# FFN-down on one Trainium2 core: column sums formed by transfers into a ring, and 8, 8, 8, 5 seven-product blocks in place of 7, 7, 7, 4

## The chip, the cores and the metric

The kernel runs on one core of one Trainium2 chip. The metric is the device time of a run in microseconds (us), the median of several runs. Three runs of the kernel before gave 1180.41, 1181.60 and 1181.63 us. A separate execution was taken by the hardware profiler; every time of an instruction below is from that one.

## The reference

One layer of a decoder trunk on 256 tokens of width 2048, in float32. The change lies in the channel mixer, a squared-ReLU MLP with a hidden width of 8192:

```python
h2 = rms_norm(x, mlp_norm[i])
x = x + jnp.square(jax.nn.relu(h2 @ w_ffn_up[i])) @ w_ffn_down[i]
gate = jax.nn.sigmoid(rms_norm(x, ple_norm[i]) @ w_ple_gate[i])
x = x + gate * (p[i] @ w_ple_proj[i])
```

What is timed is the whole layer; what is changed is the product with `w_ffn_down`, (256 x 8192) by (8192 x 2048).

## The kernel before

**Precision.** TensorE multiplies in a reduced float32 format (fp32r). Each operand is therefore split into a high part, its rounding (ScalarE, ACT below), and a low part, the rest (VectorE, DVE below: operand minus high part). A product is three matmuls: high by high, high by low, low by high. `split_sb` (L172, L173) does this for 512 columns, `halves_of` (L1240, L1241) for a panel of 1024: two ACT instructions of 512 columns and one DVE instruction of 1024. Their results are called `wh_...` and `wl_...`, or `wad` for one tile that holds both parts.

**Tiling of FFN-down.** The hidden width is worked in two halves (`hf`), the output width in two halves of 1024 columns (`pair`), so there are four *sweeps*, called d00, d01, d10, d11 by `hf` and `pair`. d00 and d01 follow each other, then comes the up-product of the second half, then d10 and d11. A sweep makes 16 *visits* (`kp`), each to 256 hidden rows: two row tiles of 128, by two column blocks of 512. With the two token tiles of 128 a visit is a product of 2 x 2 blocks. The weight blocks are w11, w12 (first row tile, column blocks one and two), w21, w22 (second row tile). The activations are a11, a12, a21, a22.

- A *plain* visit makes the usual eight block products, 24 matmuls of 128 x 512 (`prod`, L1229 to L1231).
- A *square* makes seven products, 21 matmuls, by Winograd's form of Strassen's scheme. For it the DVE forms four sums of the weight blocks (L1269 to L1272: t1 = w12 - w11, t3 = w22 - w12, t2 = t3 + w11, t4 = w21 - t2, in a tile `td`), and sums of the activations (s1 to s4, in `S`, made once per half in `activation_sums`). Their split parts are the tiles `..b` (w21, w22), `..c` (t1, t3), `..d` (t2, t4) and `wad` (w11) of a visit, `11b` being tile b of visit 11.

Before, the squares are the visits 1, 3, 5, 7, 9, 11, 13 of three sweeps and 1, 3, 7, 11 of the last. The seven products are collected in eight PSUM banks, and at the last square some of them are added to the residual stream `xr` by the DVE (`add`, L1249); four more banks are added at the sweep's end.

**Buffers and queues.** A visit loads two panels of 512 KB (`load_raw`, L158, names `raw_d...`), issued on SyncE's queue (SP) in order. Six buffers hold panels: a load waits until the last reader of an earlier panel has ended. The split parts go to three buffers `wh` and `wl` (`..a`, `..b`, `..c`), two buffers for `..d`, and one for `wad`; they come free when TensorE (PE) has made the last matmul that reads them. The order of the instructions on each engine is written out by a scheduler at build time, with `tc.high_priority` around the splits; at run time each engine takes its list strictly in order.

Of the kernel before, what the change touches and what calls it, by code (L numbers as in the profile page):

```python
# [9 lines left out]
F32 = mybir.dt.float32  # L10
F32R = mybir.dt.float32r
# [29 lines left out]
def trunk(  # L41
# [1114 lines left out]
    def inv_ms():  # L1156
        ss2 = rms_stat(xr, "n2")
        nc.vector.tensor_scalar(s2, ss2, 1.0 / D, NORM_EPS, op0=ALU.mult, op1=ALU.add)
        nc.vector.reciprocal(s2, s2)

    h3_box = []

# [22 lines left out]

    SEVEN = (1, 3, 5, 7, 9, 11, 13)
    s_slots = (0, 2, 5)

    def activation_sums(box, kp, r):

        i = SEVEN.index(kp)
        if i % 2 == 0:
            st = a8(s_slots[i // 2], f"S{kp}", F32R) if i < 6 else fp.tile([128, 1024], F32R, tag="S", name=f"S{kp}")
            box[kp] = box[SEVEN[min(i + 1, len(SEVEN) - 1)]] = st
# [5 lines left out]
        nc.vector.tensor_tensor(s3, a11, a21, op=ALU.subtract)  # L1202
# [4 lines left out]
    def down_sweep(hf, pair, ys, sboxes, hooks=(), between=None, seven=SEVEN):  # L1207

        nm = f"d{hf}{pair}"
        hooks = dict(hooks)  # L1210
# [12 lines left out]
        left = dict(todo)  # L1223

        def prod(n, a_, w_):
            first, last = left[n] == todo[n], left[n] == 1
            left[n] -= 1
            (ah, al), (wh, wl) = a_, w_
            nc.tensor.matmul(banks[n], ah, wh, start=first, stop=False)  # L1229
            nc.tensor.matmul(banks[n], ah, wl, start=False, stop=False)  # L1230
            nc.tensor.matmul(banks[n], al, wh, start=False, stop=last)  # L1231

        def halves_of(src, name, own=False):

            pool, kw = (fp, dict(bufs=2)) if own else (wp, {})
            wh = pool.tile([128, 1024], F32R, tag="graw" if own else "wh", name=f"wh_{name}", **kw)
            wl = pool.tile([128, 1024], F32R, tag="graw" if own else "wl", name=f"wl_{name}", **kw)
            with tc.high_priority(20000):
                for c in range(2):
                    nc.scalar.activation(wh[:, c * 512 : c * 512 + 512], src[:, c * 512 : c * 512 + 512], AF.Copy)  # L1240
                nc.vector.tensor_tensor(wl, src, wh.bitcast(F32), op=ALU.subtract)  # L1241
# [6 lines left out]
        def add(tt, c, src):  # L1248
            nc.vector.scalar_tensor_tensor(xs(tt, c), src, s2[:, tt : tt + 1], xs(tt, c), op0=ALU.mult, op1=ALU.add)  # L1249

        for q, kp in enumerate(((0, 2, 1, 4, 3, *range(5, 16)) if hf else (0, 2, 1, 4, 3, 6, 5, 8, 7, 10, 9, 12, 11, 14, 13, 15)) if pair else range(16)):
            if q in hooks:
                hooks[q]()
            y, j = ys[kp // 2], kp % 2 * 512
            a11, a21, a12, a22 = ((y[:, j + i * 128 : j + i * 128 + 128], y[:, 1024 + j + i * 128 : 1152 + j + i * 128]) for i in range(4))
            rx, ry = (load_raw(w_down[pair, hf * 32 + 2 * kp + i], 1024, f"{nm}_{kp}_{i}") for i in range(2))
            if kp in seven:
                i = SEVEN.index(kp)
                st = sboxes[kp][:, i % 2 * 1024 : i % 2 * 1024 + 1024]
                s1, s2_, s3, s4 = ((st[:, c * 128 : c * 128 + 128], st[:, 512 + c * 128 : 640 + c * 128]) for c in range(4))  # L1260
                t_ = a8(1, f"t{nm}_{kp}")
                t1, t3, t2, t4 = (t_[:, c * 512 : c * 512 + 512] for c in range(4))
                wa = fp.tile([128, 1024], F32R, tag="wa", name=f"wa{nm}_{kp}")
                w11 = wa[:, 0:512], wa[:, 512:1024]
                with tc.high_priority(20000):
                    split_sb(*w11, rx[:, 0:512])
                w21, w22 = halves_of(ry, f"{nm}_{kp}b")
                with tc.high_priority(20000):
                    nc.vector.tensor_tensor(t1, rx[:, 512:1024], rx[:, 0:512], op=ALU.subtract)  # L1269
                    nc.vector.tensor_tensor(t3, ry[:, 512:1024], rx[:, 512:1024], op=ALU.subtract)  # L1270
                    nc.vector.tensor_tensor(t2, t3, rx[:, 0:512], op=ALU.add)
                    nc.vector.tensor_tensor(t4, ry[:, 0:512], t2, op=ALU.subtract)  # L1272
                w1, w3 = halves_of(t_[:, 0:1024], f"{nm}_{kp}c")
                w2, w4 = halves_of(t_[:, 1024:2048], f"{nm}_{kp}d", True)
                for n, a_, w_ in (("1", a11, w11), ("2", a12, w21), ("3", s4, w22), ("5", s1, w1), ("7", s3, w3), ("6", s2_, w2), ("4", a22, w4)):
                    prod(n, a_, w_)
            else:
                w11, w12 = halves_of(rx, f"{nm}_{kp}a")
                for n, a_, w_ in (("2", a11, w11), ("4", a21, w11), ("3", a11, w12), ("x", a21, w12)):
                    prod(n, a_, w_)  # L1280
                w21, w22 = halves_of(ry, f"{nm}_{kp}b")
                for n, a_, w_ in (("2", a12, w21), ("4", a22, w21), ("3", a12, w22), ("x", a22, w22)):
                    prod(n, a_, w_)
            if kp == seven[-1]:
                u = fp.tile([128, 512], F32, tag="r", bufs=2, name=f"u{nm}")
                with tc.high_priority(20000):
                    add(0, 0, b1)
                    nc.scalar.activation(u, b1, AF.Copy)
                    nc.vector.tensor_tensor(u, b6, u, op=ALU.add)
                    add(0, 1, b5)  # L1290
                    add(1, 1, b5)
                    add(0, 1, u)
                    nc.vector.tensor_tensor(u, b7, u, op=ALU.add)
                add(1, 0, u)
                add(1, 1, u)
                if between is not None:
                    between()
        for n, tt, c in (("2", 0, 0), ("4", 1, 0), ("3", 0, 1), ("x", 1, 1)):
            with tc.high_priority(30000):
                add(tt, c, banks[n])  # L1300

    def ffn_half(hf):
# [26 lines left out]
        if hf == 0:  # L1329
            down_sweep(hf, 1, ys, sboxes)  # L1330
        else:
            down_sweep(hf, 1, ys, sboxes, {5: keep, 8: keep, 11: keep, 14: keep}, lambda: [h3_part("ple_norm", n) for n in range(2)], (1, 3, 7, 11))
            for n in range(2, 4):
                h3_part("ple_norm", n)

    ffn_half(0)
    ffn_half(1)
    h3 = h3_box[0]


    praw = load_raw(pT.rearrange("p a t -> p (a t)"), 512, "pT")
    ph, pl = (fp.tile([128, 512], F32R, tag=nm, name=nm) for nm in ("ph", "pl"))
    split_sb(ph, pl, praw[:, 0:512])
    pp = [a8(1 + tt, f"pp{tt}") for tt in range(2)]
    for n in range(4):
# [74 lines left out]
def _layout(i):  # L1420
# [13 lines left out]
    def ktiles(w):  # L1434
# [30 lines left out]
        "w_ffn_down": a["w_ffn_down"][0].reshape(64, 128, 2, 1024).transpose(2, 0, 1, 3),  # L1465
# [24 lines left out]
```

## Time and profile before

| what | value |
|---|---|
| median of three runs | 1181.6 us |
| the profiled execution, its device time | 1180.25 us |
| span of the profile | 1178.2 us |
| PE busy | 1162.5 us, 99% |
| DVE busy | 873.3 us, 74% |
| ACT busy | 709.3 us, 60% |
| moved by DMA | 216.81 MB |

The profile lists, for each engine, when every instruction ran, how long, and what ended the idle time before it. "PEld" is the weight load of TensorE, which runs beside the matmuls. "x365" is a count of instructions. A matmul's row gives 0.39 us, but the next one starts before it ends, so its cost is read from one start to the next. The same is done for the DVE and ACT, whose rows overlap a little too.

### The profile page before, as it was taken

The page shows a single profiled execution, that of the slowest core. Times are in us where ns is not written, and L with a number is a line of the kernel's source. Part 1 is how long each engine was busy: PE and PEld are TensorE (multiplying, and loading weights), DVE is VectorE, ACT ScalarE, POOL GpSimd, SP SyncE. Part 2 cuts the span into 40 slices and gives each one's busy share as a digit, 9 for nine tenths or more (in the row PEclk, how much of TensorE's full clock was granted, in tenths as well). Part 3 has the DMA queues.
Part 4 walks back from the last instruction along what each step waited for, and adds up shares of the span by engine and source line. Part 5 has one row for each costly group of instructions (what it writes and reads, how often), then busy time and mean ns, then how long its engine had stood idle before and what let it go on. Part 6 is the DMA issues. An engine that isn't in the chain of part 4 may idle for free.

```text
span 1178.2 us, 17287 instructions
## 1 busy us (share of the span) xinstructions
PE 1162.5 (99%) x6419; PEld 973.4 (83%) x6419; DVE 873.3 (74%) x1188; ACT 709.3 (60%) x1309; POOL 13.7 (1%) x73
## 2 busy tenths in 40 slices
PE   8999999999999999999999999999999999999997
PEld 8787777788887888888888888888888888888886
DVE  7786996964656666767988987676668879788543
ACT  7776848676545565555665664555556655568543
POOL 2100000000000000000000000000000000000000
PEclk9999999999999999999999999999999999999999
DMA  7464343354465555555556556555555555767511
GB/s 290 154 202 146 135 140 119 119 179 157 160 203 178 177 182 196 184 192 200 187 204 212 198 202 209 186 191 191 185 195 190 202 205 195 290 233 249 197 56 72
DMA packets 60756, 216.81 MB, mean 184 GB/s; under 512 B 6784, under 2 KB 7552, under 8 KB 60288
## 3 DMA queue, kind: packets, MB, share of 16 engines
q1 hardware_dynamic: 60240, 214.99, 52.5%
q8 instruction: 50, 0.82, 0.3%
q10 hardware_dynamic: 432, 0.73, 0.2%
q14 instruction: 34, 0.28, 0.1%
HBM read 213.59 MB, written 2.10 MB: 183 GB/s over the span
## 4 chain that ended last, share of the span: by engine, by line
PE 96%; ACT 1%; DVE 1%; DMA 0%; issue 0%; SPq 0%; POOL 0%; DVEq 0%; POOLq 0%
PE u_w L1112 20%; PE u_w L1117 10%; PE d_b L1231 7%; PE d_b L1229 7%; PE d_b L1230 7%; PE d_w L1231 2%; PE d_w L1229 2%; PE d_w L1230 2%; PE gt_b L242 2%; PE gt_b L241 2%; PE gt_b L238 2%; PE zk_b L241 1%; PE zk_b L242 1%; PE o_b L241 1%; PE o_b L242 1%; PE zv_b L238 1%
## 5 line engine op out<-in xcount | busy, mean ns | idle before, releaser
L1112 PE MATMUL u_w<-h,wh_u 128*128 128x512 f32 x1024 | 321.9, 395 | 0.0
L167 ACT ACTIVATE wh_u<-raw_u 128x512 fp32r<-128x512 f32 x256 | 147.5, 623 | 160.9 <-issue 98.2
L168 DVE TENSOR_TENSOR wl_u<-raw_u,wh_u 128x1024 fp32r<-128x1024 f32 x128 | 156.6, 1224 | 105.2 <-ACT wh_u L167 103.5
L1117 PEld LDWEIGHTS u_w<-h,wl_u 128*128 128x128 f32 x1024 | 192.4, 188 | 45.4
L1117 PE MATMUL u_w<-h,wl_u 128*128 128x256 f32 x1024 | 201.4, 278 | 0.0
L1112 PEld LDWEIGHTS u_w<-h,wh_u 128*128 128x128 f32 x1024 | 156.0, 189 | 0.1
L168 DVE TENSOR_TENSOR wl_gt<-raw_gt,wh_gt 128x1024 fp32r<-128x1024 f32 x24 | 29.4, 1224 | 23.2 <-ACT wh_gt L167 23.2
L167 ACT ACTIVATE wh_gt<-raw_gt 128x512 fp32r<-128x512 f32 x48 | 28.0, 638 | 23.1 <-PE gt_b L242 14.4
L241 PE MATMUL gt_b<-wh_gt,h 128*128 128x512 f32 x96 | 37.3, 389 | 0.0
L242 PE MATMUL gt_b<-wh_gt,h 128*128 128x512 f32 x96 | 37.3, 389 | 0.0
L168 DVE TENSOR_TENSOR wl_o<-raw_o,wh_o 128x1024 fp32r<-128x1024 f32 x16 | 19.6, 1222 | 12.9 <-ACT wh_o L167 9.9
L167 ACT ACTIVATE wh_o<-raw_o 128x512 fp32r<-128x512 f32 x32 | 18.4, 623 | 16.3 <-issue 8.5
L167 ACT ACTIVATE wh_zp<-raw_zp 128x512 fp32r<-128x512 f32 x32 | 18.6, 623 | 15.7 <-PE zp_b L242 7.2
L168 DVE TENSOR_TENSOR wl_zk<-raw_zk,wh_zk 128x1024 fp32r<-128x1024 f32 x16 | 19.4, 1220 | 10.4 <-ACT wh_zk L167 10.4
L241 PE MATMUL zk_b<-wh_zk,hTh 128*128 128x512 f32 x64 | 25.2, 394 | 1.4 <-ACT wh_zk L167 1.4
L241 PE MATMUL zv_b<-wh_zv,hTh 128*128 128x512 f32 x64 | 26.0, 406 | 0.0
L167 ACT ACTIVATE wh_zk<-raw_zk 128x512 fp32r<-128x512 f32 x32 | 18.4, 622 | 12.4 <-PE zv_b L242 4.0
L241 PE MATMUL zp_b<-wh_zp,hTh 128*128 128x512 f32 x64 | 25.7, 401 | 0.0
L238 PE MATMUL gt_b<-wl_gt,h 128*128 128x512 f32 x96 | 25.7, 389 | 0.0
L168 DVE TENSOR_TENSOR wl_zv<-raw_zv,wh_zv 128x1024 fp32r<-128x1024 f32 x16 | 19.4, 1218 | 8.2 <-ACT wh_zv L167 7.4
L241 PE MATMUL zr_b<-wh_zr,hTh 128*128 128x512 f32 x64 | 25.4, 397 | 0.0
L242 PE MATMUL zp_b<-wh_zp,hTl 128*128 128x512 f32 x64 | 25.0, 391 | 0.0
(840 smaller groups left out, 2963.9 us busy)
## 6 DMA issues: line engine op xcount, KB each, us to landing
raw_u<-in_w_ffn_up_dram SPq DMA_DIRECT2D x128, 512.0 KB, 3.5
raw_d<-in_w_ffn_down_dram SPq DMA_DIRECT2D x128, 512.0 KB, 4.3
raw_gt<-in_w_ple_gate_dram SPq DMA_DIRECT2D x24, 512.0 KB, 3.5
raw_zk<-in_w_in_dram SPq DMA_DIRECT2D x16, 512.0 KB, 3.7
raw_zr<-in_w_in_dram SPq DMA_DIRECT2D x16, 512.0 KB, 3.3
raw_zv<-in_w_in_dram SPq DMA_DIRECT2D x16, 512.0 KB, 3.3
raw_zp<-in_w_in_dram SPq DMA_DIRECT2D x16, 512.0 KB, 3.2
raw_o<-in_w_out_dram SPq DMA_DIRECT2D x16, 512.0 KB, 4.2
```

What stands on the lines that cost most here:

```text
L167: nc.scalar.activation(wh[:, a * 512 : (a + 1) * 512], raw[:, a * 512 : (a + 1) * 512], AF.Copy)
L168: nc.vector.tensor_tensor(wl, raw, wh.bitcast(F32), op=ALU.subtract)
L238: nc.tensor.matmul(banks[tt], ah[:, ts_], halves[a][1], start=False, stop=last)
L241: nc.tensor.matmul(banks[tt], ah[:, ts_], halves[a][0], start=i + a == 0, stop=False)
L242: nc.tensor.matmul(banks[tt], al[:, ts_], halves[a][0], start=False, stop=False)
L1112: nc.tensor.matmul(bank[:, ct, :].rearrange("p (s t) -> p s t", s=2), wh[:, cs[ct]], hl, start=k == 0, stop=False, skip_group_check=True,)
L1117: nc.tensor.matmul(bank[:, ct, 0:T], wl[:, cs[ct]], hl[:, 0, :], start=False, stop=k == 15, skip_group_check=True)
L1229: nc.tensor.matmul(banks[n], ah, wh, start=first, stop=False)
L1230: nc.tensor.matmul(banks[n], ah, wl, start=False, stop=False)
L1231: nc.tensor.matmul(banks[n], al, wh, start=False, stop=last)
```

## The change

- **Layout of the weights.** `w_ffn_down` is laid out so that one panel holds a column block, with the lower row tile first: panel c = 0 is (w21, w11), panel c = 1 is (w22, w12). A square loads the whole first panel, and of the second only w22 (256 KB).
- **A sum by transfers.** GpSimd's queue (POOL) issues two transfers of 256 KB per square (`begin_sum`): w12 into a slot of a ring of four, then w11 with an adding transfer over it. The slot then holds p1 = w11 + w12. Four sums are begun ahead of the first FFN half; after each square the sum for the fourth next one is begun.
- **Signs.** The second column block is computed with its sign turned, so that p1 can stand where t1 stood. Some adds therefore use `ns2` = -`s2`, and s3 has its sign turned.
- **In place.** t2 = p1 - w22 is written over the ring's slot (L1304 of the new kernel). One subtraction of 1024 columns (L1306) makes (w21 - t2, w11 - t2) over the first raw panel. So a square has on the DVE two subtractions in place of four sums, the splits of w22 and p1 go to the tile `..b`, that of t2 to `wad`, and the tile `..a` holds w21 and w11.
- **Squares and order.** Squares are 1, 3, 4, 6, 8, 9, 11, 13 in three sweeps and 1, 3, 6, 9, 11 in the last; d01 visits in the order 0, 2, 1, 5, 3, 4, 7, 6, 10, 8, 9, 12, 11, 14, 13, 15, d11 in 0, 2, 1, 4, 3, 5 to 15. `SEVEN` grows by one, so one more activation sum is made per half.

```diff
-    SEVEN = (1, 3, 5, 7, 9, 11, 13)
+    SEVEN = (1, 3, 4, 6, 8, 9, 11, 13)
...
+    ring = a8(1, "ring")
...
+            squares_of[hf, pair] = (1, 3, 6, 9, 11) if last else SEVEN
...
+    def begin_sum():
+
+        n = len(begun)
+        if n < len(in_line):
+            hf, pair, kp = in_line[n]
+            nc.gpsimd.dma_start(slot(n), w_down[pair, hf * 16 + kp, 1, :, 1, :])
+            nc.gpsimd.dma_start(slot(n), w_down[pair, hf * 16 + kp, 0, :, 1, :], accum_op=ALU.add)
+            begun.append(n)
...
-            rx, ry = (load_raw(w_down[pair, hf * 32 + 2 * kp + i], 1024, f"{nm}_{kp}_{i}") for i in range(2))
+            rx, ry = (panel(kp, c, f"{nm}_{kp}_{c}", 1 if c and kp in seven else 2) for c in range(2))
...
                 with tc.high_priority(20000):
-                    split_sb(*w11, rx[:, 0:512])
-                w21, w22 = halves_of(ry, f"{nm}_{kp}b")
-                with tc.high_priority(20000):
-                    nc.vector.tensor_tensor(t1, rx[:, 512:1024], rx[:, 0:512], op=ALU.subtract)
-                    nc.vector.tensor_tensor(t3, ry[:, 512:1024], rx[:, 512:1024], op=ALU.subtract)
-                    nc.vector.tensor_tensor(t2, t3, rx[:, 0:512], op=ALU.add)
-                    nc.vector.tensor_tensor(t4, ry[:, 0:512], t2, op=ALU.subtract)
-                w1, w3 = halves_of(t_[:, 0:1024], f"{nm}_{kp}c")
-                w2, w4 = halves_of(t_[:, 1024:2048], f"{nm}_{kp}d", True)
+                    split_sb(*w22, ry[:, 0:512])
+                    split_sb(*w1, p1)
+                    nc.vector.tensor_tensor(t2, p1, ry[:, 0:512], op=ALU.subtract)
+                    t43 = rx.rearrange("p (r n) -> p r n", r=2)
+                    nc.vector.tensor_tensor(t43, t43, t2.unsqueeze(1).to_broadcast([128, 2, 512]), op=ALU.subtract)
+                    split_sb(*w2, t2)
+                w4, w3 = halves_of(rx, f"{nm}_{kp}d", True)
...
+                begin_sum()
```

The scheduler writes other lists from this. The first place is the DVE's list in sweep d00 around square 13, before. `td_13` are the four sums of square 13, `wl_d_12a` the low part of tile a of visit 12, `wad` the low part of w11.

```order
L1241 TENSOR_TENSOR wl_d_11d<-td_11_5885,wh_d_11d 128x1024
L1241 TENSOR_TENSOR wl_d_11c<-td_11_5885,wh_d_11c 128x1024
L1269 TENSOR_TENSOR td_13_5971<-raw_d_13_0_5967 128x512
L1270 TENSOR_TENSOR td_13_5971<-raw_d_13_1_5969,raw_d_13_0_5967 128x512
L1271 TENSOR_TENSOR td_13_5971<-td_13_5971,raw_d_13_0_5967 128x512
L1241 TENSOR_TENSOR wl_d_12a<-raw_d_12_0_5929,wh_d_12a 128x1024
L173 TENSOR_TENSOR wad_13_5972<-raw_d_13_0_5967,wad_13_5972 128x512
L1241 TENSOR_TENSOR wl_d_12b<-raw_d_12_1_5931,wh_d_12b 128x1024
L1272 TENSOR_TENSOR td_13_5971<-raw_d_13_1_5969,td_13_5971 128x512
L1241 TENSOR_TENSOR wl_d_13b<-raw_d_13_1_5969,wh_d_13b 128x1024
L1241 TENSOR_TENSOR wl_d_13d<-td_13_5971,wh_d_13d 128x1024
L1241 TENSOR_TENSOR wl_d_13c<-td_13_5971,wh_d_13c 128x1024
```

The same place in the changed kernel:

```order
L1270 TENSOR_TENSOR wl_d_11d<-raw_d_11_0_5909,wh_d_11d 128x1024
L1270 TENSOR_TENSOR wl_d_13a<-raw_d_13_0_5995,wh_d_13a 128x1024
L173 TENSOR_TENSOR wl_d_13b<-raw_d_13_1_5997,wh_d_13b 128x512
L173 TENSOR_TENSOR wl_d_13b<-ring,wh_d_13b 128x512
L1304 TENSOR_TENSOR ring<-ring,raw_d_13_1_5997 128x512
L1270 TENSOR_TENSOR wl_d_14a<-raw_d_14_0_6053,wh_d_14a 128x1024
L1306 TENSOR_TENSOR raw_d_13_0_5995<-raw_d_13_0_5995,ring 128x1024
L173 TENSOR_TENSOR wad_13_5999<-ring,wad_13_5999 128x512
L1270 TENSOR_TENSOR wl_d_14b<-raw_d_14_1_6055,wh_d_14b 128x1024
L1270 TENSOR_TENSOR wl_d_13d<-raw_d_13_0_5995,wh_d_13d 128x1024
```

Before, the sums of square 13 stand ahead of the splits of visit 12, the visit before it. Now the subtraction of square 13 (L1306) stands behind the split of visit 14, the visit after it, and the last reader of raw panel 11_0 is `wl_d_11d`, of 13_0 `wl_d_13d`.

The second place is PE's list at the same square, before, from the first product of square 13 on:

```order
L1229 MATMUL d_w_5411<-wad_13_5972,y_5001 128x512
L1230 MATMUL d_w_5411<-wad_13_5972,y_5001 128x512
L1231 MATMUL d_w_5411<-wad_13_5972,y_5001 128x512
L1229 MATMUL d_b_5407<-wh_d_13b,y_5001 128x512
L1230 MATMUL d_b_5407<-wl_d_13b,y_5001 128x512
L1231 MATMUL d_b_5407<-wh_d_13b,y_5001 128x512
L1229 MATMUL d_b_5409<-wh_d_13b,S_5200 128x512
L1230 MATMUL d_b_5409<-wl_d_13b,S_5200 128x512
```

In the changed kernel, from the sixth product's first matmul (on `wad_13`) on:

```order
L1258 MATMUL d_b_5425<-wh_d_14a,y_5226 128x512
L1258 MATMUL d_w_5429<-wad_13_5999,S_5012 128x512
L1259 MATMUL d_b_5425<-wl_d_14a,y_5226 128x512
L1260 MATMUL d_b_5425<-wh_d_14a,y_5226 128x512
L1258 MATMUL d_b_5425<-wh_d_14a,y_5226 128x512
L1259 MATMUL d_b_5425<-wl_d_14a,y_5226 128x512
L1260 MATMUL d_b_5425<-wh_d_14a,y_5226 128x512
L1258 MATMUL d_b_5427<-wh_d_14b,y_5226 128x512
L1258 MATMUL d_b_5428<-wh_d_14b,y_5226 128x512
L1259 MATMUL d_w_5429<-wad_13_5999,S_5012 128x512
L1260 MATMUL d_w_5429<-wad_13_5999,S_5012 128x512
```

Before, PE takes a square's products whole and one after another. Now matmuls of the next plain visit (14a, 14b) stand between the first matmul on `wad_13` and its two others.

The third place is the loads on SP's queue, in the changed kernel; 15_1 and 14_0 are panels of visits 15 and 14.

```order
L158 DMA raw_d_14_1_6055<-in_w_ffn_down_dram 128x1024
L158 DMA raw_d_15_0_6091<-in_w_ffn_down_dram 128x1024
L158 DMA raw_d_15_1_6093<-in_w_ffn_down_dram 128x1024
L158 DMA raw_d_14_0_6053<-in_w_ffn_down_dram 128x1024
L158 DMA raw_d_0_0_6139<-in_w_ffn_down_dram 128x1024
```

Panel 14_0 takes the buffer of panel 11_0, so it waits for `wl_d_11d`, and stands behind 15_1, which waits for `wl_d_12b`, the DVE instruction just ahead of that.

More of the change, by code (lines that the diff above doesn't have):

```diff
@@ L1205, in activation_sums, with slot, summed, down_sweep @@
         split_sb(st[:, 0:512], st[:, 512:1024], t_[:, 0:512])
-    def down_sweep(hf, pair, ys, sboxes, hooks=(), between=None, seven=SEVEN):
+    ring = a8(1, "ring")
+    squares_of = {}
+    visits_of = {}
+    for hf in range(2):
+        for pair in range(2):
+            last = hf + pair == 2
+            squares_of[hf, pair] = (1, 3, 6, 9, 11) if last else SEVEN
+            visits_of[hf, pair] = (0, 2, 1, 4, 3, *range(5, 16)) if last else (range(16), (0, 2, 1, 5, 3, 4, 7, 6, 10, 8, 9, 12, 11, 14, 13, 15))[pair]
+    in_line = [(*hp, kp) for hp, visits in visits_of.items() for kp in visits if kp in squares_of[hp]]
+    begun = []
+    def slot(n):
+        return ring[:, n % 4 * 512 : n % 4 * 512 + 512]
+    def begin_sum():
[5 more added lines that the diff above has]
+            begun.append(n)
+    def summed(*square):
+        return slot(in_line.index(square))
+    def down_sweep(hf, pair, ys, sboxes, hooks=(), between=None):
         nm = f"d{hf}{pair}"
+        seven, visits = squares_of[hf, pair], visits_of[hf, pair]
         hooks = dict(hooks)
@@ L1246, in xs, with add, panel @@
             return xr[tt][:, o : o + 512]
-        def add(tt, c, src):
-            nc.vector.scalar_tensor_tensor(xs(tt, c), src, s2[:, tt : tt + 1], xs(tt, c), op0=ALU.mult, op1=ALU.add)
-        for q, kp in enumerate(((0, 2, 1, 4, 3, *range(5, 16)) if hf else (0, 2, 1, 4, 3, 6, 5, 8, 7, 10, 9, 12, 11, 14, 13, 15)) if pair else range(16)):
+        def add(tt, c, src, scale=s2):
+            nc.vector.scalar_tensor_tensor(xs(tt, c), src, scale[:, tt : tt + 1], xs(tt, c), op0=ALU.mult, op1=ALU.add)
+        def panel(kp, c, name, rows):
+            return load_raw(w_down[pair, hf * 16 + kp, c, :, 0:rows].rearrange("p r n -> p (r n)"), rows * 512, name)
+        for q, kp in enumerate(visits):
             if q in hooks:
@@ L1283, in down_sweep @@
+                for n, a_, w_ in (("3", a12, w22), ("x", a22, w22), ("3", a11, w12), ("x", a21, w12)):
                     prod(n, a_, w_)
-            if kp == seven[-1]:
+            if kp == max(seven):
                 u = fp.tile([128, 512], F32, tag="r", bufs=2, name=f"u{nm}")
```

39 lines of the change are left out of this document (23 added, 16 removed).

## The prediction

> **What bounds the kernel now.** I read the page's head and its chain first, then TensorE's waits, then the sweeps as stretches of the span, and last the instructions of one period of a sweep. The page's busy line and its chain:
>
> ```profile
> span 1178.2 us, 17287 instructions
> ...
> PE 1162.5 (99%) x6419; PEld 973.4 (83%) x6419; DVE 873.3 (74%) x1188; ACT 709.3 (60%) x1309; POOL 13.7 (1%) x73
> ...
> PE 96%; ACT 1%; DVE 1%; DMA 0%; issue 0%; SPq 0%; POOL 0%; DVEq 0%; POOLq 0%
> ```
>
> TensorE (PE) is 96% of the chain that ended last. In the list of its waits, of nine rows the first and the last are
>
> ```profile
> PE zk_b L241 <- ACT wh_zk L167: 1.4, 1, 1.4
> ...
> PE um L854 <- ACT R L818: 0.4, 1, 0.4
> ```
>
> and none of the nine names a tile of FFN-down (`d_b`, `d_w`). So in the sweeps PE waits for nothing, and time is made of matmuls alone. The stretches of d00, d01, d10 and of d11 with what follows it (columns: us, then busy time and count of PE, its loads, DVE, ACT, POOL, then clock and DMA):
>
> ```profile
> 557.90:640.20 82.30, 82.30 (x365) 68.18 (x364) 71.35 (x83) 49.66 (x86) 0.00 (x0) 1.00 0.58 202
> 640.20:722.50 82.30, 82.30 (x364) 68.12 (x363) 72.22 (x82) 49.12 (x85) 0.00 (x0) 1.00 0.57 199
> 900.90:983.20 82.30, 82.30 (x366) 68.14 (x365) 71.34 (x83) 49.64 (x86) 0.00 (x0) 1.00 0.55 197
> 983.20:1073.00 89.80, 89.80 (x408) 74.00 (x407) 76.59 (x87) 58.40 (x108) 0.00 (x0) 1.00 0.70 251
> ```
>
> A full sweep has 7 x 21 + 9 x 24 = 363 matmuls, so one costs 82.30 / 363 = 0.227 us at full clock. But the DVE is busy 87% there, so what it and the loads must deliver is nearly as much as PE takes. One period of d00, a plain visit and a square, on the DVE:
>
> ```profile
> 604.16 0.69 DVE L1269 TENSOR_TENSOR td<-raw_d 128x512 f32<-128x512 f32 x1
> 604.77 0.68 DVE L1270 TENSOR_TENSOR td<-raw_d,raw_d 128x512 f32<-128x512 f32 x1
> 605.49 0.69 DVE L1271 TENSOR_TENSOR td<-td,raw_d 128x512 f32<-128x512 f32 x1
> 606.10 1.22 DVE L1241 TENSOR_TENSOR wl_d_10a<-raw_d,wh_d_10a 128x1024 fp32r<-128x1024 f32 x1
> 607.23 0.68 DVE L173 TENSOR_TENSOR wad<-raw_d,wad 128x512 fp32r<-128x512 f32 x1
> 607.84 1.22 DVE L1241 TENSOR_TENSOR wl_d_10b<-raw_d,wh_d_10b 128x1024 fp32r<-128x1024 f32 x1
> 608.97 0.68 DVE L1272 TENSOR_TENSOR td<-raw_d,td 128x512 f32<-128x512 f32 x1
> 609.58 1.22 DVE L1241 TENSOR_TENSOR wl_d_11b<-raw_d,wh_d_11b 128x1024 fp32r<-128x1024 f32 x1
> 610.71 1.22 DVE L1241 TENSOR_TENSOR wl_d_11d<-td,wh_d_11d 128x1024 fp32r<-128x1024 f32 x1
> 613.10 1.23 DVE L1241 TENSOR_TENSOR wl_d_11c<-td,wh_d_11c 128x1024 fp32r<-128x1024 f32 x1 [1.18 <-ACT wh_d_11c L1240]
> 614.36 0.69 DVE L1269 TENSOR_TENSOR td<-raw_d 128x512 f32<-128x512 f32 x1
> ```
>
> From start to start an instruction of 512 columns takes 0.61 us (604.77 less 604.16), one of 1024 columns 1.13 (607.23 less 606.10). The period lasts 614.36 - 604.16 = 10.20 us, with 1.18 idle. What freed the buffer of tile 11c, and when PE wants it:
>
> ```profile
> 611.43 0.39 PE L1231 MATMUL d_b<-wh_d_10a,y 128*128 128x512 f32 x1
> 616.42 0.39 PE L1229 MATMUL d_w<-wh_d_11c,S 128*128 128x512 f32 x1
> 611.92 1.15 ACT L1240 ACTIVATE wh_d_11c<-td 128x512 fp32r<-128x512 f32 x2 [1.59 <-PE d_b L1231]
> ```
>
> From the start of the last matmul on a tile to the ACT instruction that overwrites it lie 611.92 - 611.43 = 0.49 us. Tile 11c, the latest of its square, is done at 613.10 + 1.23 = 614.33 and wanted at 616.42 + 0.23 = 616.65: 2.3 us of slack. The chain of PE is closed by a margin of about that much.
>
> **The matmuls.** Four plain visits become squares, at three matmuls each: 12 x 0.227 = 2.7 us off PE's list. This is the whole gain; the time before holds no wait in the sweeps that could go too.
>
> **The work of DVE and ACT.** A square cost the DVE five instructions of 512 and three of 1024, 5 x 0.61 + 3 x 1.13 = 6.4 us; now four and three (the double subtraction taken as one of 1024, reading one operand twice: the same elements as a split), 5.8. A plain visit stays at 2.3. A sweep goes from 7 x 6.4 + 9 x 2.3 = 65.5 to 8 x 5.8 + 8 x 2.3 = 64.8 us, on top of the same eleven adds: no more in total. ACT has seven instructions per square as before against four of a plain visit: three more per sweep, 3 x 0.6 us into 33 idle us (82.3 less 49.7). The eighth activation sum of a half (five short DVE instructions and one of ACT) falls in the up-product; if it were uncovered, it is 2 x about 2 us, bounded by its four quarter-width sums and one 512 split at no more than 0.69 each. `ns2` and the signs cost nothing beside that.
>
> **The sums by transfers.** Each square adds two transfers of 256 KB, one behind the other, and drops 256 KB from its load. The nearest rows for 256 KB, and the 512 KB one:
>
> ```profile
> wa<-in_wa_up_dram SPq DMA_DIRECT2D x2, 256.0 KB, 2.7
> ...
> raw_pT<-in_pT_dram SPq DMA_DIRECT2D x1, 256.0 KB, 4.2
> ```
>
> A sum then takes between 2 x 2.7 and 2 x 4.2 = 8.4 us if adding costs as copying does, and it is begun four squares ahead, which is at least four squares and a plain visit or two, some 24 us of PE. Hidden with room; twice the price is hidden too. POOL's queue holds nothing else in the FFN (its busy time in the four stretches is 0.00), so nobody stands behind its waits. [...]
>
> **The reloads, where I expect the loss.** Before, a square's raw panels came free early, after the four sums, the last of which (608.97) stands 7.5 us ahead of PE's 616.42. Now the first panel is overwritten in place and read until the square's last split, `wl_d_11d`. In the new lists panel 14_0 waits for that, and the split of 14a stands on the DVE ahead of square 13's double subtraction. So there is a loop over a square and a plain visit: the load L, two ACT halves 1.15, then on the DVE 14a 1.13, double subtraction 1.13, t2's split 0.61, 14b 1.13, 13d 1.22, which frees the next panel: L + 6.4. PE's period is 21 + 24 = 45 matmuls, 45 x 0.227 = 10.2, so L may be 3.8 us. The loads in d00 (all 22 of one stretch, then one issued 2.0 us behind another one, then one of four in a burst):
>
> ```profile
> DMA to landing us min/median/max: 3.4/5.2/7.4
> ...
> L158 SPq DMA_DIRECT2D raw_d<-in_w_ffn_down_dram x1: 328/328/328, 629.3 to 629.3; - x1
> ...
> DMA to landing us min/median/max: 4.2/4.2/4.2
> ...
> L158 SPq DMA_DIRECT2D raw_d<-in_w_ffn_down_dram x1: 327/327/327, 619.3 to 619.3; - x1
> ...
> DMA to landing us min/median/max: 5.7/5.7/5.7
> ```
>
> A load alone takes 3.4: no loss. Panel 14_0 is issued some 1.1 us behind 15_1, between the second and the third case; I take 4.8, a loss of 1.0 us. The same happens at 14_0 in d00, d01 and d10: 3.0 us, with bounds of 0 (L = 3.4) and 3 x (5.7 - 3.8) = 5.7. [...]
>
> **Two squares in a row.** 3 and 4, 8 and 9 now follow each other in three sweeps: six pairs. A pair asks 2 x 5.8 = 11.7 us of the DVE in 42 x 0.227 = 9.5 of PE. The new lists put matmuls of the next plain visit between, so it is not a loss of 2.2 each: for 8 and 9 in d00 the DVE needs 5.8 us from one `..d` split to the next where PE's list has 24 matmuls, 5.4. I take 0.25 per pair, 1.5 us, with bounds of 0 and, for a pair whose tile `..b` also waits for a buffer (0.49 + two ACT halves 1.15, of which about half is hidden), 1.1 each, 6.6.
>
> **Single squares.** The chain from the last matmul on tile a of a plain visit to the same of the next one is 0.49 + 1.15 (ACT) + 0.61 + 0.61 + 1.13 + 1.13 + 0.61 + 1.13 + 1.22 (DVE: p1's split, t2, a, double subtraction, t2's split, b, d) and 9 matmuls, 2.04: 10.1 with nothing for the hand-over between engines, 10.25 with 0.03 (613.10 less the end of ACT at 613.07) at each of four. PE's own is 10.2. I take 0.5 us for all seventeen, bounds 0 and 2.
>
> **The sum.** -2.7 + 3.0 + 1.5 + 0.5 = +2.3 us. Against the profiled execution's 1180.25 us (2.05 outside its span) that is 1182.55; the median of the runs shown, 1181.6, lies 1.35 above it, so the forecast is 1183.9.
>
> **The rivals.**
>
> - *All waits hidden.* If reloads land in 3.8 us and the lists were written with a true picture of DVE and ACT, PE stays dense: -2.7, 1178.9. For it: no wait of PE in any sweep now, and lists that fill every gap with other matmuls. Against it: the 2.3 us of slack is used up, and a median load takes 5.2. It is faster than before only while all waits stay under 0.4 us.
> - *Partly hidden.* Waits of 0.4 to 2 us, 1179.3 to 1180.9.
> - *The DVE becomes the bound in the pairs and the reloads are as in a burst.* 6.6 + 5.7 + 2 - 2.7 = +11.6, 1193. It decides where a tile `..b` waits for its buffer in each pair. For it: 87% busy in the sweep. Against: the DVE's sum did not grow.
> - *The change doesn't do what it says:* sums arrive late since an adding transfer is several times slower than a copy. From 24 us per sum on, each of 29 squares waits; at 30 us it is 29 x 6, far above any range. No row shows an adding transfer, so a small chance stays.
>
> **How the numbers follow.** About 0.2% (2.4 us) is what a measurement of this kernel can tell from no change. All hidden: 0.18, the only case of faster. Partly hidden 0.13, all within 0.2%. My forecast, waits of 2 to 8 us: 0.47, of which the part under 5.1 us of waits, 0.22, is still within 0.2%, and 0.25 slower. The bound DVE: 0.19, slower. Late sums: 0.03, slower. So faster 0.18, same 0.35, slower 0.47. The forecast's own range is 1180.9 to 1186.9. The range for 8 in 10 takes in the full gain at the low end and leaves out late sums and the upper part of the bound DVE: 1178.6 to 1190.
>
> **What would show it.** Right: PE's waits name `d_b` and `d_w`, held by DVE splits `..d` and `wad` and by ACT on raw panels, some 5 us in all, most in the second half of the sweeps d00, d01 and d10; SP's waits name `wl_d_11d`. Matmul starts elsewhere stay 0.227 apart. The reload step is wrong if the stretches d00 to d10 shrink to 360 x 0.227 = 81.6 us each. The steps on the DVE are wrong if its instruction of 1024 columns with a repeated operand takes much over 1.22, or its others lengthen beside the transfers. The whole is wrong if POOL's transfers are waited for.

## The result, and the profile after

The changed kernel takes 1193.3 us (four runs, 1192.57 to 1194.49); the kernel before, run beside it, 1181.6 us (1180.41 to 1182.38). The ratio is 1.0101, with a 95% interval of 1.0083 to 1.0118: slower by 11.7 us. The forecast was 1183.9, with a range up to 1190. The profiled execution took 1193.56 us; from its page:

```profile
span 1191.8 us, 17365 instructions
...
PE 1171.1 (98%) x6407; PEld 968.5 (81%) x6407; DVE 875.2 (73%) x1194; ACT 708.5 (59%) x1323; POOL 56.9 (5%) x131
```

DVE and ACT do what they did (873.3 and 709.3 us before), and PE makes 12 matmuls fewer. The time is idle time and slowed matmuls of PE. The four sweeps as stretches, with the columns of the prediction; the last one ends here at the first matmul of the projection behind it:

```profile
559.08:645.60 86.52, 84.24 (x363) 66.47 (x361) 71.96 (x82) 49.85 (x91) 11.50 (x16) 1.00 0.70 213
645.60:730.92 85.32, 84.37 (x362) 66.21 (x360) 72.05 (x82) 48.77 (x89) 10.62 (x15) 1.00 0.71 221
909.25:994.47 85.22, 84.16 (x362) 66.41 (x361) 71.95 (x82) 49.81 (x91) 11.47 (x16) 1.00 0.72 216
994.47:1083.45 88.98, 87.44 (x390) 70.20 (x389) 75.47 (x86) 55.24 (x104) 1.45 (x2) 1.00 0.70 234
```

The first three took 82.3 us each and should have come down by three matmuls, 0.7 us, to 81.6. Of the span's 13.7 us more, 4.2, 3.0 and 2.9 lie in these, 2.3 in the last sweep with the small product behind it, and 1.15 ahead of the first sweep (it begins at 559.08, before at 557.93). This last part is at 30 to 60 us, where the granted clock was 0.94, and 1.00 before; of the kernels below e2, e7 and e10 have it (mean clock of the span 0.997, 0.993 and 0.997, and 0.997 here) and the others do not (0.998 or 0.999; 0.995 in e5, by a later stretch), with the same instructions there, so it is no effect of the change. With the matmuls saved (0.7 us a sweep), the waits come to 4.9, 3.7, 3.6 and 3.0: 15.2 us, where the prediction had 5.0. What PE and its weight loads waited for in FFN-down, in the list of waits (total us, times, longest):

```profile
PE d_w L1258 <- ACT wad L172: 2.8, 4, 1.0
PE d_w L1259 <- DVE wad L173: 2.0, 3, 1.5
...
PE d_b L1258 <- ACT wh_d_10b L1269: 0.6, 2, 0.3
```

```profile
PEld d_w L1259 <- DVE wad L173: 7.2, 13, 1.9
PEld d_w L1258 <- ACT wad L172: 6.2, 9, 1.4
```

`wad` holds t2's split, product 6. One such place, square 11 of d00, first on PE, then on ACT:

```profile
619.64 0.39 PE L1260 MATMUL d_w<-wh_d_11b,S 128*128 128x512 f32 x1
620.98 0.50 PE L1258 MATMUL d_w<-wad,S 128*128 128x512 f32 x1 [0.96 <-ACT wad L172]
621.33 0.40 PE L1258 MATMUL d_b<-wh_d_12a,y 128*128 128x512 f32 x1
621.57 0.40 PE L1259 MATMUL d_b<-wl_d_12a,y 128*128 128x512 f32 x1
```

```profile
611.79 1.14 ACT L1269 ACTIVATE wh_d_11a<-raw_d 128x512 fp32r<-128x512 f32 x2
616.49 0.63 ACT L172 ACTIVATE wh_d_11b<-raw_d 128x512 fp32r<-128x512 f32 x1 [3.56 <-issue]
617.02 0.62 ACT L172 ACTIVATE wh_d_11b<-ring 128x512 fp32r<-128x512 f32 x1
617.62 1.15 ACT L1269 ACTIVATE wh_d_12a<-raw_d 128x512 fp32r<-128x512 f32 x2
619.78 0.63 ACT L1269 ACTIVATE wh_d_12b<-raw_d 128x512 fp32r<-128x512 f32 x1 [1.01 <-DMA raw_d<-in_w_ffn_down_dram]
620.32 0.61 ACT L172 ACTIVATE wad<-ring 128x512 fp32r<-128x512 f32 x1
```

Two things hold ACT up. It stands idle for 3.56 us until it may write tile 11b; the page has no releaser ("issue"), but the tile's buffer is that of 10a, whose last matmul started shortly before, at 616.0:

```profile
L1260 PE MATMUL d_b<-wh_d_10a,y x4: 389/389/389, 610.5 to 616.0; 128*128 128x512 f32 x4
```

So 11b begins 0.48 us behind that, and p1's split, t2 and `wad` follow on it. The same distance, 0.43 to 0.48 us behind the last matmul on tile a of the plain visit ahead, is found at 19 of the 29 squares, all but one of those that ACT reached idle. Second, `wad` stands in ACT's list behind half of 12b, whose panel was late; its load took 6.1 us:

```profile
L158 SPq DMA_DIRECT2D raw_d<-in_w_ffn_down_dram x1: 327/327/327, 613.5 to 613.5; - x1
...
  ACT wh_d_12b L1269: 1.0, 1
...
DMA to landing us min/median/max: 6.1/6.1/6.1
```

### The profile page after: what moved, and what is told of

Its sections match the earlier page's. It is cut to its first block, busy times and chain, and to the rows that moved or that the text cites. A ratio compares the mean times of both kernels' runs of the same rounds, so it can differ in the third digit from the quotient of the medians.

```text
span 1191.8 us, 17365 instructions
## 1 busy us (share of the span) xinstructions
PE 1171.1 (98%) x6407; PEld 968.5 (81%) x6407; DVE 875.2 (73%) x1194; ACT 708.5 (59%) x1323; POOL 56.9 (5%) x131
## 5 line engine op out<-in xcount | busy, mean ns | idle before, releaser
L1228 POOL DMA_DIRECT2D ring<-in_w_ffn_down_dram x29 | 16.6, 574 | 604.0 <-DVE wad L173 528.1
L1306 DVE TENSOR_TENSOR raw_d<-raw_d,ring 128x1024 f32<-128x1024 f32 x29 | 35.4, 1222 | 0.5
L1229 POOL DMA_DIRECT2D ring<-in_w_ffn_down_dram x29 | 25.2, 869 | 111.4 <-DMA ring<-in_w_ffn_down_dram 107.0
```

What stands on the lines that cost most here:

```text
L1228: nc.gpsimd.dma_start(slot(n), w_down[pair, hf * 16 + kp, 1, :, 1, :])
L1229: nc.gpsimd.dma_start(slot(n), w_down[pair, hf * 16 + kp, 0, :, 1, :], accum_op=ALU.add)
L1306: nc.vector.tensor_tensor(t43, t43, t2.unsqueeze(1).to_broadcast([128, 2, 512]), op=ALU.subtract)
```

## The experiments

Two theories came out of this reading. The first was that late panels (reload) explain the larger waits. When it accounted for 3 us only, the second took its place: the chain of each square begins too late, because tile b waits for its buffer. The rivals throughout: the DVE's work where two squares follow each other, and the traffic of the sums. The table has the times as ratios to the kernel before on the same chip (its medians there were 1179.95 to 1181.62 us, so medians of different rows are compared by their ratios), and from each profile the stretches d00, d01, d10 and, from the start of d11 to the first matmul of `gt_b`, the last one.

| kernel | median us | ratio (95%) | d00 | d01 | d10 | last |
|---|---|---|---|---|---|---|
| before | 1181.6 | 1 | 82.3 | 82.3 | 82.3 | 99.2 |
| changed | 1193.3 | 1.0101 (1.0083 to 1.0118) | 86.5 | 85.3 | 85.2 | 101.5 |
| e1 panel not overwritten | 1190.7 | 1.0090 (1.0075 to 1.0105) | 84.9 | 84.2 | 85.0 | 102.9 |
| e2 no later sums | 1189.1 | 1.0077 (1.0062 to 1.0092) | 85.1 | 84.2 | 84.9 | 100.3 |
| e3 new path, 7 7 7 4 | 1186.0 | 1.0051 (1.0034 to 1.0068) | 83.7 | 83.7 | 83.7 | 100.6 |
| e4 old path, 8 8 8 5 | 1180.3 | 1.0004 (0.9995 to 1.0013) | 82.0 | 82.0 | 81.9 | 101.1 |
| e5 b and d swapped | 1193.1 | 1.0101 (1.0085 to 1.0116) | 82.5 | 82.5 | 82.5 | 103.1 |
| e6 `wad` first | 1199.7 | 1.0158 (1.0143 to 1.0173) | 89.3 | 86.7 | 85.8 | 104.7 |
| e7 e3, swapped | 1189.5 | 1.0073 (1.0058 to 1.0088) | 82.3 | 82.3 | 82.3 | 101.1 |
| e8 e5, 7 panels | 1185.2 | 1.0044 (1.0027 to 1.0061) | 82.5 | 82.5 | 82.5 | 104.3 |
| e9 swapped in three sweeps | 1186.0 | 1.0044 (1.0031 to 1.0057) | 82.8 | 82.5 | 82.5 | 104.3 |
| e10 e9, 8 8 8 4 | 1183.5 | 1.0020 (1.0011 to 1.0030) | 82.7 | 82.5 | 82.5 | 101.4 |
| e11 old path, 8 8 8 4 | 1180.4 | 0.9992 (0.9983 to 1.0001) | 81.9 | 82.0 | 82.0 | 100.3 |
| e12 e3, four tiles in turn | 1182.1 | 1.0014 (1.0005 to 1.0024) | 82.3 | 82.3 | 82.3 | 100.4 |

**e1: the double subtraction into a tile of its own.**

```diff
-                    t43 = rx.rearrange("p (r n) -> p r n", r=2)
+                    t43 = fp.tile([128, 1024], F32, tag="t43", bufs=1, name=f"t43{nm}_{kp}")
...
-                w4, w3 = halves_of(rx, f"{nm}_{kp}d", True)
+                w4, w3 = halves_of(t43, f"{nm}_{kp}d", True)
```

> The double subtraction writes a tile of its own (the one of 4 KB that the activation sums and the norm used, which now take a tile of the down-product), so that a square's first raw panel is free after that subtraction and not after the last split; the lists of ACT and DVE stay as in the changed kernel. Theory (reload): the waits at squares 11 and 13 of the first three sweeps and at 9 of the last, some 7 us of the 15, come from panels that are released by the last split; 4 to 7 us come back, 1186 to 1189 us, and the loads of 14_0 and 12_0 are no longer released by wl_d_..d. Rival (pairs, DVE bound): nothing to gain, 1192 to 1194. Rival (traffic of the sums): nothing to gain either, 1192 to 1194.

The three sweeps got back 1.6, 1.1 and 0.2 us, 2.9 in all, at squares 11 and 13 where the theory had it, and not the 4 to 7 expected; 9.3 us of waits stay there. The last sweep, where the theory had a gain at square 9, grew by 1.4. So reload is real and is the smaller part.

**e2: no sums after the first four.**

```diff
                 prod(n, a_, w_)
-                begin_sum()
```

> Leaves out the transfers of the sums after the first four: the later squares work on what the ring holds, so products 5, 6, 4 and 7 of 25 squares are of other numbers; every instruction of PE, ACT, DVE and the loads by SP stays. Theory (reload): releases are the same, only the landing of a panel gets shorter (median 4.6 back to about 4.3): 1 to 2.5 us, 1191 to 1192.5. Rival (traffic of the sums): the loads beside two sums, now 5 to 7.6 us long, fall to 3.5 to 5.5 and 5 us or more come back, 1185 to 1188. Rival (pairs): 1193.

The kernel of e2 leaves out 25 sums, so what it computes is not the layer; only its time counts. The three sweeps got back 1.4, 1.1 and 0.3, 2.8 us at the same squares, and the last sweep 1.3. The loads of d00 and d01, of the changed kernel, then of this one:

```profile
raw_d<-in_w_ffn_down_dram SPq DMA_DIRECT2D x42, 512.0 KB, 5.0
ring<-in_w_ffn_down_dram POOLq DMA_DIRECT2D x31, 256.0 KB, 4.7
```

```profile
raw_d<-in_w_ffn_down_dram SPq DMA_DIRECT2D x42, 512.0 KB, 4.2
```

A panel is late only where it is released late and then takes 0.8 us longer beside the sums; taking away either one is enough. Neither touches the other 9 us.

The 1.3 us of the last sweep are another matter. They lie at its square 9. The panel that 9a waited for took 6.8 us to land in the changed kernel and 4.4 in e2. It was issued 38.3 us into the sweep, when no sum was under way: the last one of the changed kernel had landed at 24.1, and e2 has none there. Three loads ahead of it on the same queue, issued at 32.8, stands one of 1 MB, `fn` (`final_norm`). That load took 8.5 us in the changed kernel and 5.1 in e2, but 6.3 before and 9.1 and 9.5 in e4 and e11, which have no sums at all. So these 1.3 us are not shown to be a price of the sums.

**e3 and e4: each half of the change alone.** e3 has the new data path with the squares and visits of before; e4 the data path of before with the new ones.

```diff
-    SEVEN = (1, 3, 4, 6, 8, 9, 11, 13)
+    SEVEN = (1, 3, 5, 7, 9, 11, 13)
```

> The new data path (ring, double subtraction in place, sums by transfers) with the squares and visits of before, 7, 7, 7 and 4, none two in a row; 12 matmuls more, 2.7 us. Theory (reload): a single square loses as much as in the changed kernel, 25 of 29 squares and no pairs: waits of some 10 to 13 us, 1191 to 1194. Rival (pairs, DVE bound): the waits go, and the time is that of before or a little under, 1180 to 1184. Rival (traffic): waits of 10 to 13 us, as by the reload.

> The data path of before (sums formed on the DVE, panels free early, no transfers of sums) with the squares and visits of the changed kernel, 8, 8, 8 and 5; 12 matmuls fewer than before, 2.7 us. Theory (reload): no panel is held, so only the pairs cost, some 0.5 us each at most: 1179 to 1183. Rival (pairs, DVE bound): 2 x 6.4 us of DVE against 9.5 of PE in each of six pairs, 2 us or more each: 1190 or more. Rival (traffic): as the theory.

e4 shows that the pairs alone cost little: 82.0 us per sweep, one wait of 0.2 us in each at 9d. It gained 0.3 us in each of the three sweeps and gave 1.9 back in the last, where PE waited 1.9 us for tile 11d. e3 came out between the theories: no pair, and still 1.4 us lost in each sweep. Its first sweep, and PE around its square 5:

```profile
558.53:642.20 83.67, 83.67 (x365) 67.52 (x364) 70.44 (x80) 47.88 (x88) 10.10 (x14) 1.00 0.73 222
```

```profile
588.66 0.39 PE L1258 MATMUL d_b<-wh_d_6a,y 128*128 128x512 f32 x1
588.88 0.39 PE L1259 MATMUL d_b<-wl_d_6a,y 128*128 128x512 f32 x1
589.15 0.50 PE L1259 MATMUL d_b<-wl_d_5d,y 128*128 128x512 f32 x1
589.49 0.40 PE L1260 MATMUL d_b<-wh_d_5d,y 128*128 128x512 f32 x1
589.73 0.39 PE L1259 MATMUL d_w<-wl_d_5d,S 128*128 128x512 f32 x1
```

PE is busy 83.67 of 83.67 us and no wait is listed, yet the starts tell of one: 0.27 us to the matmul on `wl_d_5d` in place of 0.227, then 0.34 to the next, then 0.24. This comes at every one of the seven squares, at the same place, 0.2 us each. A period of a square and a plain visit takes 10.38 us in place of 10.2: the loop through b's buffer. In the same period, the start of the chain on ACT and the steps behind it on the DVE (p1's split, t2, the double subtraction):

```profile
582.28 0.63 ACT L172 ACTIVATE wh_d_5b<-raw_d 128x512 fp32r<-128x512 f32 x1 [2.86 <-PE d_b L1260]
```

```profile
583.55 0.69 DVE L173 TENSOR_TENSOR wl_d_5b<-ring,wh_d_5b 128x512 fp32r<-128x512 f32 x1
584.27 0.69 DVE L1304 TENSOR_TENSOR ring<-ring,raw_d 128x512 f32<-128x512 f32 x1
585.00 1.23 DVE L1306 TENSOR_TENSOR raw_d<-raw_d,ring 128x1024 f32<-128x1024 f32 x1
```

ACT is idle for 2.86 us until PE lets go of tile 4a. Each of the DVE's steps here needs what the one before it has done, and they start 0.72 and 0.73 us apart, not 0.61.

**e5, e6 and e7: the buffer of b.** e5 lets b and d change places, e7 does so in e3; e6 leaves the buffers and moves `wad` to the front of the lists.

```diff
-                wh, wl = (wp.tile([128, 1024], F32R, tag=hl, name=f"{hl}_{nm}_{kp}b") for hl in ("wh", "wl"))
+                wh, wl = (fp.tile([128, 1024], F32R, tag="graw", bufs=2, name=f"{hl}_{nm}_{kp}b") for hl in ("wh", "wl"))
...
-                w4, w3 = halves_of(rx, f"{nm}_{kp}d", True)
+                w4, w3 = halves_of(rx, f"{nm}_{kp}d")
```

> In a square the tiles of b (the lower half panel and the sum) and of d (the double subtraction's two) change places: b goes into the pair of tiles of the square's own, d into the three that the plain visits take in turn. No instruction is added or taken away. Theory (buffers of b): b's first ACT instruction waits until PE is done with tile a of the plain visit ahead (0.43 to 0.48 us behind its last matmul in most squares of the changed kernel), and t2, wad and d all stand behind it; with the swap that wait goes, ACT and DVE fall back to writing a square's tiles in order, 9 to 14 us come back, and the time is 0.997 to 1.001 of before. Rival (the DVE's work in the pairs, 11.7 us against 9.5): the work is the same, the six pairs go on costing 1 us or more each, 1.004 or more of before. Rival (reload): panels are still overwritten in place, 3 us come back at most from an earlier d, 1.007.

```diff
-                    split_sb(*w2, t2)
+                    with tc.high_priority(40000):
+                        split_sb(*w2, t2)
```

> Only the order of the lists: t2's split (wad) is given the highest rank, so that ACT and DVE do it ahead of the double subtraction and ahead of the next visit's panel. Theory (buffers of b): the chain still begins at the buffer of b; wad comes one or two DVE instructions (1.13 us each) earlier and d later by 0.61, so the waits on wad go and some on d come: 2 to 5 us back, 1.006 to 1.008 of before. Rival (order alone): if the lists' order is the cause and not the buffers, 9 us or more come back, 1.003 or less. Rival (DVE's work in the pairs): unchanged, 1.009 to 1.011.

> The kernel of run e3 (new data path, squares 7, 7, 7 and 4, none in a row) with b and d swapped. Theory (buffers of b): the 0.155 us and the slower pace behind it that every square lost there, some 0.2 us each, go: 0.998 to 1.001 of before. Rival (traffic of the sums, or the DVE's work): the same 5 us as there, 1.004 to 1.006.

By their times e5 and e7 speak against the theory: 1.0101 and 1.0073. Their sweeps speak for it. Those of e5:

```profile
563.44:645.96 82.52, 82.27 (x363) 67.29 (x361) 73.10 (x82) 50.15 (x90) 11.54 (x16) 1.00 0.75 224
645.96:728.44 82.48, 82.23 (x362) 67.30 (x360) 72.19 (x81) 49.27 (x88) 11.52 (x16) 1.00 0.77 227
906.77:989.29 82.52, 82.28 (x362) 67.29 (x361) 73.09 (x82) 50.15 (x90) 11.51 (x16) 1.00 0.76 228
```

9.5 us of the 12.2 are back with the same instructions on every engine, though in other orders; in e7 the sweeps are dense again. What e5 lost, it lost elsewhere: 1.5 us more in the last sweep, where the kept gate panels share b's new tiles, and 6.3 ahead of the first sweep, in the product with `w_out` (54.4 us in place of 48.1 from its first matmul to the first of the up-product). There PE waited, ACT had waited before it, and the granted clock was 0.95 and 0.70 over two stretches of 10 us, after 1.00 in the one ahead of them:

```profile
PE h2t L1134 <- DVE x L1071: 4.2, 2, 3.7
```

```profile
ACT wh_d_1b L172 <- DMA ring<-in_w_ffn_down_dram: 5.9, 1, 5.9
```

```profile
335.00:345.00 10.00, 6.59 (x30) 5.11 (x28) 2.83 (x3) 3.51 (x7) 3.57 (x4) 0.95 1.00 261
345.00:355.00 10.00, 9.72 (x35) 7.85 (x36) 5.13 (x7) 3.50 (x7) 0.00 (x0) 0.70 0.56 177
```

b's new tile is free from the start, so the scheduler put the split of the first sum, `wh_d_1b`, among those of `w_out`, 200 us early. On the chip ACT stood there for the ring's transfers with the splits of `w_out` behind it.

e6 shows that the late place of `wad` in the lists is not the cause by itself: with `wad` first, the next visit's panel is split later, PE waits for `wl_d_9a` and `wh_d_14a` as well, and by the ratios 6.7 us are added. The theory's own 2 to 5 us back were wrong as well: in a chain that begins late, what is moved ahead moves something else behind. Other orders were not run.

**e8, e9 and e10: a version without the side effects.** e8 adds a seventh panel buffer to e5 (`raw2`, four in place of three). e9 keeps the swap to three sweeps and leaves out the first square; e10 also has four squares in the last sweep.

```diff
+                own = hf + pair < 2 and (hf, pair, kp) != in_line[0]
+                pool, kw = (fp, dict(bufs=2)) if own else (wp, {})
```

> b and d swapped and one buffer more for raw panels, seven (in the 4 KB that the activation sums' and the norm's tile leaves, which take one of the square's own). Theory (buffers of b): panels are early enough once d is; within 1 us of run e5. Rival (reload): late panels still cost the 3 us that runs e1 and e2 got back, so this run is 2 to 3 us below run e5.

> b and d change places as in run e5, but in the first three sweeps alone, and not in the very first square, so that ACT's list no longer holds the split of the first sum among those of w_out, and the tiles that the kept gate panels use in the last sweep are as in the changed kernel. Theory (buffers of b, and two side effects of the swap): the three sweeps stay at the 82.5 us of run e5 (86.5, 85.3 and 85.2 in the changed kernel), PE's wait of 3.7 us at the transposes of w_out and the half clock behind it go, the last sweep is as in the changed kernel, 2.3 us above before: 1.0015 to 1.004 of before. Rival (the first sums' transfers beside w_out's panels make that wait, whatever ACT's list): it stays, 1.006 or more. Rival (DVE's work in the pairs): 1.006 or more, too, but in the sweeps.

> Run e9 with four squares in the last sweep (1, 3, 6, 11) in place of five; three matmuls more, 0.7 us. Theory: the last sweep's fifth square costs more than its 0.7 us there, since the kept gate panels share DVE and ACT; 0.5 to 1.5 us below run e9. Rival (the last sweep loses by the data path, not by the fifth square): 0.7 us above run e9.

In e8 the sweeps are those of e5: with b's chain early, panels are no longer late, and a seventh buffer adds nothing there. It is 7.9 us below e5 by the medians, 5.0 in the profiled executions, since PE did not wait at `w_out`: in e8 the activation sums use b's tiles during the up-product, so that the split of the first sum comes only at 538.6 us. In e9 that wait is gone too and the three sweeps stay. Its d00 is 0.3 us longer than that of e5, and this lies at square 1, the one that kept its old tiles: there the matmul on `wl_d_1d` comes 0.05 us late and the next one 0.11 later still, as in e3. The miss is the last sweep, 104.3 us in place of the 101.5 expected; e10 got 2.9 of it back without the fifth square, more than expected. The code of e9 for that sweep is that of the changed kernel, but the scheduler's lists are not: in e9 ACT splits the first kept gate panel ahead of 7a and of square 6's `wad`, and `fn` is issued 27.5 us into the sweep in place of 32.8. Which of this costs the 2.8 us was not found. So it is not shown either that e5 lost its 1.5 us there by the shared tiles.

**e11: the pairs with the data path of before, four squares last.**

```diff
-            ... lambda: [h3_part("ple_norm", n) for n in range(2)], (1, 3, 7, 11))
+            ... lambda: [h3_part("ple_norm", n) for n in range(2)], (1, 3, 6, 11))
```

> Run e4 (data path of before, the pairs) with four squares in the last sweep (1, 3, 6, 11); nine matmuls fewer than before, 2.0 us. Theory: three sweeps of 82.0 us as in run e4, 0.3 below before each, and a last sweep as before: 0.9 us below before, 0.9985 to 1.0, the only version here that is not slower. Rival (the last sweep's wait of 2.05 us in run e4 is not of the fifth square): it stays, 1.0005 to 1.0015.

The ratio is as forecast: 0.9992, from 0.9983 to 1.0001. It is the only version whose median is under that of before on its chip; the interval does not exclude no change. The account behind it holds in part only. The three sweeps gained 1.0 us, but the last one took 100.3 us and not the 99.2 of before, and the profiled execution has the same span as before, 1178.2 us.

**e12: one tile more for b to go to.** In e3, `halves_of` and b take four tiles in turn.

```diff
+        if len(turns) % 4 == 0:
+            return [fp.tile([128, 1024], F32R, tag=hl + "4", name=f"{hl}_{name}") for hl in ("wh", "wl")]
+        return [wp.tile([128, 1024], F32R, tag=hl, name=f"{hl}_{name}") for hl in ("wh", "wl")]
```

> The kernel of run e3 (new data path, 7, 7, 7 and 4 squares, b and d in their places) with one tile more of high and of low parts for the plain visits and b in turn, four in place of three, in the room that the eighth activation sum and the norm's tile leave. Theory (buffers of b): b's split no longer waits for tile a of the plain visit ahead, and the three sweeps fall from the 83.7 us of run e3 to 82.3 to 82.5, as with the swap; 4 us less than run e3, 1.001 to 1.003 of before. Rival (the swap helped since it moved d or changed the lists, not by the tile that b waits for): 83.7 us per sweep stay, 1.004 to 1.006.

Its three sweeps:

```profile
557.34:639.64 82.30, 82.30 (x365) 68.13 (x364) 72.44 (x81) 49.90 (x88) 10.08 (x14) 1.00 0.77 233
639.64:721.92 82.28, 82.28 (x364) 68.13 (x363) 69.51 (x76) 47.99 (x84) 10.05 (x14) 1.00 0.75 230
900.26:982.55 82.29, 82.29 (x365) 68.14 (x364) 72.44 (x81) 49.87 (x88) 10.05 (x14) 1.00 0.78 233
```

The tiles of d are where they were, b has one more to go to, and the 1.4 us are gone in each sweep, with all sums under way. ACT no longer waits for PE before b; it begins behind its own split of 7a:

```profile
586.17 0.63 ACT L172 ACTIVATE wh_d_7b<-raw_d 128x512 fp32r<-128x512 f32 x1 [0.21 <-ACT wh_d_7a L1275]
```

So for the single squares the wait of b for its tile is the cause. One thing changed with it: the lists now have d's split ahead of the next visit's tile a, not behind it, which is worth one DVE instruction, 1.13 us. It does not carry the result, since `wl_d_7d` is done at 592.92, 4.1 us ahead of PE's first matmul on it (597.03). Whether that order alone, with three tiles, would have been enough in e3 was not run. What e12 still loses, 1.2 us, lies in the last sweep.

## Why the prediction was wrong

- **The matmuls** were right: 12 fewer, 2.7 us.
- **The work of DVE and ACT** was right: no more in total, and the double subtraction takes 1.22 us. The DVE is not the bound by its work: in e12 it is busy 72.4 of 82.3 us in d00, and PE waits for nothing in the three sweeps.
- **The sums by transfers** are hidden, as said, though slower: in the sweeps 7.9 us (595.16 to 603.02 in d00) to 11.5 (605.79 to 617.29) in place of 8.4 at most. One transfer took 4.7 us in the median, where the prediction had 2.7 to 4.2 from the rows of before. Their price is the panels' 0.8 us beside them: 5.0 in the median in the changed kernel, 4.2 in e2.
- **The reloads** were right in size and mechanism: 3.0 us forecast, 2.8 to 2.9 measured by e1 and e2. The prediction had them at panel 14_0, square 13, alone; the places were squares 11 and 13.
- **Two squares in a row:** six pairs at 0.25 = 1.5 us forecast. With b's chain out of the way (e5), the three sweeps lose 82.5 - 81.6 = 0.9 each, 0.45 per pair, 2.7 in all, where PE waits for `..d` of the pair's second square. This term was 1.2 too small.
- **Single squares** is the step that failed. The prediction had the chain right, from the last matmul on tile a of a plain visit through b, p1's split, t2 and d to the next: 10.1 to 10.25 us against PE's 10.2. It took so small a shortfall for a small cost, 0.5 us for all seventeen, at most 2. In e3, where every square is single, the period is 10.38 us and each square loses 0.2, which is 3.4 for seventeen. Two things make the difference. A step that needs the one before it started 0.72 us behind it (e3, and the prediction's own rows from 604.77 to 605.49), where the prediction put 0.61. And the waits there cost more than their length: around square 5 of e3 a matmul starts 0.045 us late, and the square loses 0.2. In the changed kernel the buffer of b and what it drags along is 9.5 us of 12.2 in the three sweeps; less reload's 2.9 this is 6.6. The twelve single squares of these sweeps make 2.4 of it at e3's rate. The other 4.2 come only where pairs and late chains share a sweep: e3 has no pairs, and e4, with the pairs and the old data path, loses 0.3 to 0.4 us a sweep. No run parts these 4.2 further.
- **The rival that came out at 1193** had the number by another route. It put 6.6 us on the pairs, where b waits for its buffer; that wait is real, but it is at most squares, single ones too, and it goes (e12, and with the pairs e5) while the DVE's work stays. Its reload of 5.7 was 2.9, its singles of 2 were more, and it had nothing for the last sweep. That its sum met the measured time is luck.
- **The last sweep** had no term of its own: it is 2.3 us longer, with 3.0 us of waits. Half of these are one wait of PE, 1.5 us at square 9, for `wad` behind a late panel. What made that panel late is open, since no sum was under way then, and so is the rest.
- **Together:** 2.9 (reload), 2.7 (pairs), 6.6 (the buffer of b) and 3.0 (last sweep) are the 15.2 us of waits that stand against the forecast's 5.0. That the change would cost time was forecast; what it costs was not.

## What to carry to other kernels

Where a tile's buffer is released by the consumer that is to be kept dense, write out the loop of release, fill and use and compare it with the period. A loop that comes out equal to the period was not free here: 10.1 to 10.25 us by the sum against 10.2, and 0.2 us lost in every period of e3. So do not put a new step behind such a release without need. Give the start of the longest chain the tile that comes free first, and see then where a scheduler puts an instruction whose buffer is free early: in e5 it stood on ACT in front of the splits of `w_out` and waited 5.9 us for a transfer.

## What the runs showed of the hardware

- In e3 a short wait of PE cost some 0.15 us more than it lasted. Around square 5 a matmul that comes 0.045 us late is followed by one that starts 0.34 us later in place of 0.227, and the few behind it start 0.23 to 0.24 apart; in all 0.2 us. The same 0.11 us in the next start stands behind waits of the changed kernel: 0.96 us at 620.98 (621.33 less 620.98 is 0.35) and 1.49 us at 1046.97 (the next start is at 1047.31). The row shows 0.50 us in place of 0.39, and the busy time counts it as work.
- Around PE's wait of 3.7 us in e5, from 341.6 to 345.3, the granted clock was 0.95 over the 10 us up to 345 and 0.70 over the 10 behind: an estimate of (0.30 x 10 + 0.05 x 10) / 0.5 = 7 us, if it was half of full speed there. Of these, 0.05 x 10 / 0.5 = 1 us lies ahead of 345, so by this estimate the clock fell at about 344, some 2.4 us into the wait. Behind the wait, matmuls of 512 columns started 0.42 to 0.43 us apart up to 350.88, and then 0.26 and 0.23: 5.6 us of slowed work from 345.28 on, which cost some 2.8 us beside the wait's 3.7.
- In the changed kernel a wait of 1.73 us (35.94 to 37.67) went with a granted clock of 1.00 up to 37.49 and of 0.50 from there to 40.91; before, the wait at the same place was 0.85 us, with 1.00 from 35 to 45. The wait of 1.49 us in the last sweep of the changed kernel left the clock at 1.00 (1040 to 1052). In e4, which has a wait of 1.9 us, the mean clock of the span is 0.998, as before, where the changed kernel has 0.997. From these runs the length of a wait that brings the clock down can't be given.
